# More Strassen pairs in a hybrid encoder block: six further gate and up pairs, an earlier feed of their weight sums, and one gate projection moved to the start

## The chip, the cores and the metric

The kernel runs on one core of a Trainium2 chip, in one launch. The metric is the device time of an execution in microseconds (us). TensorE multiplies matrices, ScalarE (ACT), VectorE (DVE) and GpSimd (POOL) work on elements, SyncE (SP) issues most transfers; ACT and POOL issue some as well. Each of them works through its own instructions in order.

## The reference, cut to what matters

One residual block over 512 frames of 1024 channels, float32:

```python
h = rmsnorm(x, norm1_w)
q, k, v, z, b_raw, a_raw, glu, gates = split(h @ w_in)      # q, k, v, z: 8 heads of 128
q, k, v = silu(causal_conv(concat(q, k, v), dn_conv_w))     # kernel of 4; then q, k l2-normalised
beta, g = sigmoid(b_raw), -exp(A_log) * softplus(a_raw + dt_bias)
o = gated_delta_rule_chunked(q, k, v, g, beta)              # recurrence over time, per head
out_a = (rmsnorm(o) * silu(z)) @ dn_w_o
c = causal_conv(ga * sigmoid(gb), cm_dw_w)                  # kernel of 31
out_b = silu(layernorm(c)) @ cm_w_pw2 + cm_b_pw2
x = x + (sigmoid(gates_a) * out_a + sigmoid(gates_b) * out_b) @ w_out
f_gate, f_up = split(rmsnorm(x, norm2_w) @ w_gate_up)       # 1024 -> 2 x 2816
x = x + (silu(f_gate) * f_up) @ w_down
return rmsnorm(x, norm_f_w)
```

## The kernel before

Activations lie with channels on the 128 partitions and the 512 frames along the free dimension. Every weight is read as float32 and split in two parts, whi and wlo (ScalarE rounds, VectorE takes the rest), and so is every activation (hh and hl). A product of one weight block is three matmuls: high by high, high by low, low by high (`split3`, line 118). `unit` (line 105 loads, 108 and 109 split) prepares 128 x 1024 weight values; its buffers raw, whi and wlo are three deep each.

Stages in order of time:

1. **Start (to 46 us).** x and the first weights come in slices. While the norm's row sums are still unknown, the first GLU products and the 16 columns for beta and decay run on un-normalized inputs uh and ul, and are scaled by the row factor rsb afterwards (`early`, lines 216 to 291). Then xt is scaled by rsb and split into hh and hl (lines 297 to 300), from which all later projections of w_in are made.
2. **Heads and gates (46 to 474 us).** Per head, three projections with a convolution of 4 (`conv4`), one for the gate z, and the preparation of the recurrence (`front`, `front2`, with a substitution `y` on GpSimd, lines 454 and 456). Projections are Python generators that give way after every eighth of a block; `count` counts these steps, eight for a projection. `step` works through a queue: a head, then some steps of `others` (GLU blocks, later the 16 output gates). Beside it run `chains`: `decays` (the cumulated decays and their matrices), and from `START + 32 * nh + ...` on the recurrence of head nh (`chain`).
3. **Output projections, w_out, second norm (474 to 616 us).**
4. **Gate and up projections, 22 pairs of 128 hidden channels.** The first F0 = 10 pairs are plain (48 matmuls of 512 columns each, `col_tile`); the last 12 are Strassen's seven products of half-size blocks (84 matmuls of 256 columns, `pair`, `hprod`). For those the activations are combined beforehand in 11 steps (`todo`), done behind the plain pairs, and the weights' combinations are four sums s1 to s4 per pair, kept in DRAM.
5. **Down projection (848 us to the end)**, also Strassen's products, with sums `wsum` of its weights' blocks.

The sums s1 to s4 are made by transfers alone. `feed` is the list of them in the order of need. `feed_one` issues one copy from SP, behind the last weight load, and, two copies later, an accumulating transfer from POOL. `fill` runs inside `unit` while `start_feed` is true, which is from count 335 on, and with it the loads of half blocks for `wsum` (`half_load`, into the tile "U" that `front` also uses), which POOL adds up:

```python
units[0] += 1
if units[0] % 3 != 2 or not gps_:
    feed_one()
if taken and units[0] % 3 != 2 and not norming[0]:
    dsums_add(*taken.pop(0))
```

`gps_` is empty in stages 4 and 5, so there every unit feeds. What is left of `wsum`'s halves is loaded by POOL in stage 4 (`dsums_to`). The compiler's scheduler orders the instructions of each engine by program order, priorities and its estimate of when operands are ready; `issue_after` and `behind` put an instruction behind a named one of its engine.

Of the kernel before, what the change touches and what calls it, by code (L numbers as in the profile page):

```python
# [6 lines left out]
F32 = mybir.dt.float32  # L7
F32R = mybir.dt.float32r
I32 = mybir.dt.int32
AF = mybir.ActivationFunctionType  # L10
# [13 lines left out]
PAD3 = 368  # L24
START = 84
ROUND = 40
# [5 lines left out]
def block_kernel(ctx, tc, a):  # L32
# [111 lines left out]

    FK, F0 = FF // 2, 10
    sums = {n: dram.tile([FF - F0, P, T], F32, name=n, bufs=1) for n in ("s1", "s2", "s3", "s4")}
# [62 lines left out]
    with tc.tile_pool(name="st", bufs=2) as st:  # L209
# [7 lines left out]
                 for p, kw in ((wp, {}), (wp, {}), (st, {}), (st, {}))]  # L217
        nc.sync.dma_start(vec, a["vec"])
        nc.scalar.dma_start(ident, a["cst"][:, 0:P])
# [5 lines left out]
        for q in range(4):  # L225
            nc.sync.dma_start(xt[:, 2 * q, :], a["xt"][2 * q])
            load(0, q)
            nc.sync.dma_start(xt[:, 2 * q + 1, :], a["xt"][2 * q + 1])
            if q == 0:
                nc.sync.dma_start(wb, a["wba"])  # L230
            for u in (1, 2):
                load(u, q)
        xtok = pa_.tile([P, NT, D], F32, name="A")
# [11 lines left out]
        wbh, wbl = wbhl[:, :, 0, :], wbhl[:, :, 1, :]  # L245
        V.tensor_copy(out=wbh, in_=wb)
        V.tensor_tensor(out=wbl, in0=wb, in1=wbh.bitcast(F32), op=ALU.subtract)

# [3 lines left out]
        for k in range(KD):  # L252
            w = vec[:, k:k + 1]
            S.activation(uh[:, k, :], xt[:, k, :], AF.Copy, scale=w)
            V.scalar_tensor_tensor(out=ul[:, k, :], in0=xt[:, k, :], scalar=w, in1=uh[:, k, :].bitcast(F32),
                                   op0=ALU.mult, op1=ALU.subtract)
            if k % 2 == 0:
                c = slice(k * P, k * P + 256)
                for raw, hi, lo in early[:3]:
                    S.activation(hi[:, c], raw[:, c], AF.Copy)  # L260
                    V.tensor_tensor(out=lo[:, c], in0=raw[:, c], in1=hi[:, c].bitcast(F32), op=ALU.subtract)
            c = slice(k * P, k * P + P)
            for (_, hi, lo), ps in zip(early[:3], eps_):
                split3(ps, (hi[:, c], lo[:, c]), uh[:, k, :], ul[:, k, :], k == 0, k == KD - 1)
            PE.matmul(bps[0:32, :], wbs[:, 32 * k:32 * k + 32], uh[:, k, :], start=k == 0, stop=False)
            PE.matmul(bps[0:16, :], wbs[:, 32 * k:32 * k + 16], ul[:, k, :], start=False, stop=k == KD - 1)
        ss = st.tile([P, 2, NT], F32, name="rms_ss", bufs=1)
# [13 lines left out]
        for k in range(KD):  # L281
            c = slice(k * P, k * P + P)
            split3(eps_[3], (hi[:, c], lo[:, c]), uh[:, k, :], ul[:, k, :], k == 0, k == KD - 1)
        def glu0(i):
            sg = tp.tile([P, T], F32, name="sg")
# [21 lines left out]
        for n in range(NT):  # L307
# [26 lines left out]
        V.scalar_tensor_tensor(out=sp, in0=ax, scalar=0.0, in1=sp, op0=ALU.max, op1=ALU.add)  # L334
        V.tensor_tensor(out=g, in0=sp, in1=nea.rearrange("p (a h) -> p a h", a=1).broadcast_to([P, NT, H]),
                        op=ALU.mult)
        V.tensor_scalar(out=eb, in0=eb, scalar1=1.0, scalar2=None, op0=ALU.add)
        V.reciprocal(out=beta, in_=eb)
        V.tensor_scalar(out=nbeta, in0=beta, scalar1=-1.0, scalar2=None, op0=ALU.mult)


# [36 lines left out]

    zall = pa_.tile([P, H, T], F32, name="A")
    junk = tp.tile([P, T], F32, name="pa", bufs=1)  # L380
# [320 lines left out]
    def decays():  # L701

        yield 2
        gps = psg.tile([P, 4, P], F32, name="g")
# [16 lines left out]
    def head(h, done):  # L721
# [14 lines left out]
        v_ = yield from v  # L736
        pz = yield from proj(24 + h)
        z_ = zall[:, h, :]
        S.activation(z_, pz, AF.Silu)


# [27 lines left out]
    while step() or chains:  # L769
        start_feed[0] = count[0] >= 335  # L770
        if nh < H and count[0] >= START + 32 * nh + sum(OTHERS[:nh]):
            chains.append([0, chain(*done[nh])])
            nh += 1
        for c in list(chains):
            if c[0] <= count[0] or not queue:
                with behind():
                    n = next(c[1], None)
                if n is None:
                    chains.remove(c)
                else:  # L780
                    c[0] = count[0] + n
# [227 lines left out]
    def some_operands(f):  # L1009
        if not ff:  # L1010
            fxs.close()
            ff.append(ctx.enter_context(tc.tile_pool(name="ff", bufs=FK)))
        for _ in range(3 if f < F0 else 2):
            if len(made) <= f:
                operands(len(made))
                made.append(1)

    def next_todo():
        if todo:
            with behind():  # L1020
                todo.pop(0)()

    for f in range(F0):
# [8 lines left out]
        sg = fq.tile([P, T], F32, name="cw", bufs=2)  # L1032
        S.activation(sg, pg, AF.Silu)
        if f:
            next_todo()
            pu = psm.tile([P, T], F32, name="mm")
# [4 lines left out]
        tt(hidden(), pu, sg, ALU.mult)  # L1041
        if f:
            next_todo()
        if f > 6:
            some_operands(f)

# [250 lines left out]
```

## Time and profile before

| | |
|---|---|
| three executions | 960.74, 963.14, 963.42 us; median 963.14 |
| profiled execution | 964.17 us, span 961.9 us, granted TensorE clock 0.998 |
| TensorE matmul busy | 98% of the span |
| VectorE, ScalarE, GpSimd busy | 76%, 55%, 37% |
| moved by transfers | 177.39 MB, mean 184 GB/s |
| stage 4, plain part | about 635 to 727.5 us |
| stage 4, Strassen pairs | 727.5 to 848.4 us |

The span is from the first to the last instruction of the profiled execution; its time is 2.3 us longer. Rows of the trace give start, length, engine, line, operation and the tiles written and read; in brackets the idle time before it and what ended it. "PEld" is TensorE's weight load, "SPq" an issue by SyncE. A DMA share is the mean busy share of the core's 16 DMA engines.

### The profile page before, as it was taken

To read this page: it belongs to the slowest core of one execution; us is meant where nothing else is said; L and a number is where in the kernel's file an instruction comes from. 1 tells how busy PE (TensorE), PEld (TensorE's weight loads), DVE (VectorE), ACT (ScalarE), POOL (GpSimd) and SP (SyncE) were. 2 spreads that over 40 slices of the span, in tenths; PEclk is the share of its full clock that TensorE was granted. 3 is DMA by queue.
4 is the path that set the end of the run, shared out by engine and by line. 5 is a ranking of instruction groups with operands and counts; after the bars stand their busy time and mean duration, and the time that the engine had idled before them with its cause. 6 is when DMAs were issued, how large, how long until landed. Compare 5 with 4: busy or idle time off the path is not lost.

```text
span 961.9 us, 14869 instructions
## 1 busy us (share of the span) xinstructions
PE 941.8 (98%) x5199; PEld 793.8 (83%) x5199; DVE 731.8 (76%) x1118; ACT 529.4 (55%) x1095; POOL 357.4 (37%) x565
## 2 busy tenths in 40 slices
PE   6999999999999999999999999999999999999996
PEld 5687888888887887888887888888889999988885
DVE  4898888988888888888477763676525887889886
ACT  6588865867856775544547232423324545556554
POOL 0323645243463327534345342245451111134034
PEclk9999999999999999999999999999999999999999
DMA  9243423133231426988897985499899556578653
GB/s 310 94 143 101 123 66 92 59 116 102 66 103 55 129 82 176 279 253 248 257 297 221 288 277 175 174 272 281 294 252 224 191 184 193 174 221 268 212 192 134
DMA packets 78298, 177.39 MB, mean 184 GB/s; under 512 B 10208, under 2 KB 19328, under 8 KB 77200
## 3 DMA queue, kind: packets, MB, share of 16 engines
q1 hardware_dynamic: 66816, 144.88, 45.4%
q0 software_dynamic: 10256, 28.89, 13.3%
q10 hardware_dynamic: 1152, 2.69, 0.7%
q8 instruction: 41, 0.67, 0.3%
q14 instruction: 33, 0.27, 0.1%
HBM read 156.22 MB, written 45.37 MB: 210 GB/s over the span
## 4 chain that ended last, share of the span: by engine, by line
PE 90%; DVE 4%; ACT 2%; POOL 2%; issue 1%; DMA 1%; SPq 0%; POOLq 0%; ACTq 0%; DVEq 0%
PE mm L118 59%; PE w L118 20%; PE g L385 1%; PE st L564 1%; PE g L418 1%; PE st L558 1%; DVE wlo L109 1%; PE b L490 1%; PE st L563 1%; PE b L496 1%; DMA gsl<-sgd 1%; POOL ss L879 1%; PE b L514 1%; PE st L552 1%; PE g L467 1%
## 5 line engine op out<-in xcount | busy, mean ns | idle before, releaser
L108 ACT ACTIVATE whi<-raw 128x1024 fp32r<-128x1024 f32 (+1 forms) x191 | 196.4, 1030 | 246.8 <-PE mm L118 151.1
L109 DVE TENSOR_TENSOR wlo<-raw,whi 128x1024 fp32r<-128x1024 f32 (+1 forms) x191 | 242.3, 1270 | 95.9 <-ACT whi L108 95.3
L118 PE MATMUL mm<-hh,whi 128*128 128x512 f32 (+1 forms) x688 | 269.9, 393 | 0.5 <-ACT whi L108 0.3
L118 PE MATMUL mm<-hl,whi 128*128 128x512 f32 (+1 forms) x688 | 264.0, 384 | 2.3 <-POOL hl L300 1.6
L118 PE MATMUL mm<-hh,wlo 128*128 128x512 f32 (+1 forms) x688 | 263.9, 384 | 0.1
L620 DVE SCALAR_TENSOR_TENSOR cps<-c,c31w,cps 128x512 f32<-128x512 f32 x240 | 180.2, 751 | 4.3
L118 PEld LDWEIGHTS mm<-hl,whi 128*128 128x128 f32 x688 | 129.9, 189 | 24.7 <-POOL hl L300 2.9
L118 PEld LDWEIGHTS mm<-hh,wlo 128*128 128x128 f32 x688 | 129.6, 188 | 23.8 <-DVE wlo L109 0.6
L118 PEld LDWEIGHTS mm<-hh,whi 128*128 128x128 f32 x688 | 129.8, 189 | 22.7 <-ACT whi L108 0.8
L949 POOL TENSOR_TENSOR fm<-fm 128x256 f32<-128x256 f32 x33 | 29.8, 904 | 113.3 <-DVE s L949 90.1
L372 DVE SCALAR_TENSOR_TENSOR acc<-mm,c4w,acc 128x511 f32<-128x511 f32 (+2 forms) x72 | 53.0, 738 | 1.9 <-ACT acc L369 1.9
L118 PE MATMUL mm<-yh,whi 128*128 128x512 f32 x128 | 50.7, 396 | 0.0
L118 PE MATMUL mm<-yl,whi 128*128 128x512 f32 x128 | 50.0, 391 | 0.6 <-DVE yl L808 0.6
L454 POOL TENSOR_TENSOR ytm<-U,y 128x60 f32<-128x60 f32 (+14 forms) x120 | 31.8, 265 | 48.6 <-DMA U<-sc 30.9
L118 PE MATMUL mm<-yh,wlo 128*128 128x512 f32 x128 | 49.8, 389 | 0.0
L118 PE MATMUL w<-hh,wlo 128*128 128x256 f32 x168 | 47.7, 284 | 0.3 <-DVE wlo L109 0.3
L118 PE MATMUL w<-hh,whi 128*128 128x256 f32 x168 | 47.6, 284 | 0.0
L118 PE MATMUL w<-hl,whi 128*128 128x256 f32 x168 | 47.5, 283 | 0.0
L118 PE MATMUL w<-wlo,fh 128*128 128x512 f32 (+1 forms) x115 | 44.3, 385 | 0.2 <-DVE wlo L109 0.2
L118 PE MATMUL w<-whi,fl 128*128 128x512 f32 (+1 forms) x115 | 44.2, 384 | 0.0
L118 PE MATMUL w<-whi,fh 128*128 128x512 f32 (+1 forms) x115 | 44.2, 384 | 0.0
L456 POOL TENSOR_TENSOR y<-y,ytm 128x60 f32<-128x60 f32 (+14 forms) x120 | 39.0, 325 | 9.4
(324 smaller groups left out, 1904.0 us busy)
## 6 DMA issues: line engine op xcount, KB each, us to landing
raw<-in_win_dram SPq DMA_DIRECT2D x61, 512.0 KB, 3.5
raw<-in_wgu_dram SPq DMA_DIRECT2D x32, 512.0 KB, 3.5
s<-in_wgu_dram SPq DMA_DIRECT2D x48, 256.0 KB, 6.2
raw<-s SPq DMA_DIRECT2D x48, 256.0 KB, 3.8
raw<-wsum SPq DMA_DIRECT2D x44, 256.0 KB, 4.0
raw<-in_wdn_dram SPq DMA_DIRECT2D x33, 256.0 KB, 3.3
s<-in_wgu_dram POOLq DMA_DIRECT2D x24, 256.0 KB, 6.9
s<-s POOLq DMA_DIRECT2D x24, 256.0 KB, 7.0
```

What stands on the lines that cost most here:

```text
L108: marked(S.activation(hi, raw, AF.Copy), "unit")
L109: marked(V.tensor_tensor(out=lo, in0=raw, in1=hi.bitcast(F32), op=ALU.subtract), "unit")
L118: marked(PE.matmul(ps, l, r, start=first and i == 0, stop=last and i == 2))
L372: marked(V.scalar_tensor_tensor(out=acc[:, s:], in0=ps[:, :T - s], scalar=c4w[:, j, k:k + 1], in1=acc[:, s:], op0=ALU.mult, op1=ALU.add))
L385: PE.transpose(ps[:, n, :], src[:, n, :], ident)
L418: PE.matmul(ps[:, n, :], kT[:, n, :], kT[:, n, :], start=True, stop=True)
L454: G.tensor_tensor(out=tm[:, :, 0:w], in0=U[:, k, :, k + 1:], in1=y[:, :, k:k + 1].broadcast_to([P, NT, w]), op=ALU.mult)
L456: last[0] = G.tensor_tensor(out=y[:, :, k + 1:], in0=y[:, :, k + 1:], in1=tm[:, :, 0:w], op=ALU.add)
L467: PE.matmul(ps[:, n, :], kT[:, n, :], qT[:, n, :], start=True, stop=True)
L490: PE.matmul(ps[:, n, 0:16], Ud[:, n, :], xc[:, n, 0:16], start=True, stop=True)
L620: V.scalar_tensor_tensor(out=acc, in0=c[:, k:k + T], scalar=c31w[:, i, k:k + 1], in1=acc, op0=ALU.mult, op1=ALU.add)
L949: return eng.tensor_tensor(out=out, in0=in0, in1=in1, op=op)
```

## The change

- The last 18 pairs instead of the last 12 are Strassen's (F0 = 4), so four sums each for six more pairs are made: 72 feeds instead of 48. `start_feed` is true from count 112 on instead of 335.
- The 11 combinations of activations go into the four plain pairs: two slots a pair, and as many at the first slot as would not fit otherwise. The hidden blocks' operands for the down projection are made from the first Strassen pair on, up to two a pair.
- Head 0's gate projection (weight block 24) runs at the start on uh and ul; its result is scaled by rsb and goes through silu after the decay inputs. Head 0 is one projection shorter.
- The load of `vec` goes from SP's queue to ACT's; the load of the 16 beta and decay columns goes behind the other first weights, and their products are made two eighths later.
- `decays` waits for 12 counts instead of 2; recurrences start at 80 instead of 84, and four counts sooner again from head 1 on.

```diff
-START = 84
+START = 80
...
-    FK, F0 = FF // 2, 10
+    FK, F0 = FF // 2, 4
...
-        nc.sync.dma_start(vec, a["vec"])
+        nc.scalar.dma_start(vec, a["vec"])
...
             nc.sync.dma_start(xt[:, 2 * q + 1, :], a["xt"][2 * q + 1])
+            for u in (1, 2):
+                load(u, q)
             if q == 0:
                 nc.sync.dma_start(wb, a["wba"])
-            for u in (1, 2):
-                load(u, q)
...
-        V.tensor_copy(out=wbh, in_=wb)
-        V.tensor_tensor(out=wbl, in0=wb, in1=wbh.bitcast(F32), op=ALU.subtract)
...
-            PE.matmul(bps[0:32, :], wbs[:, 32 * k:32 * k + 32], uh[:, k, :], start=k == 0, stop=False)
-            PE.matmul(bps[0:16, :], wbs[:, 32 * k:32 * k + 16], ul[:, k, :], start=False, stop=k == KD - 1)
+            if k == 1:
+                V.tensor_copy(out=wbh, in_=wb)
+                V.tensor_tensor(out=wbl, in0=wb, in1=wbh.bitcast(F32), op=ALU.subtract)
+            for b in [k - 2] if 1 < k < KD - 1 else [k - 2, k - 1, k] if k > 1 else []:
+                PE.matmul(bps[0:32, :], wbs[:, 32 * b:32 * b + 32], uh[:, b, :], start=b == 0, stop=False)
+                PE.matmul(bps[0:16, :], wbs[:, 32 * b:32 * b + 16], ul[:, b, :], start=False, stop=b == KD - 1)
...
+        zps = pst.tile([P, 4, P], F32, name="st").rearrange("p n t -> p (n t)")
+        hi, lo = unit(a["win"][24])
+        for k in range(KD):
+            c = slice(k * P, k * P + P)
+            split3(zps, (hi[:, c], lo[:, c]), uh[:, k, :], ul[:, k, :], k == 0, k == KD - 1)
+        zall = pa_.tile([P, H, T], F32, name="A")
...
+        with tc.issue_after(g_.ins):
+            V.tensor_tensor(out=zall[:, 0, :], in0=zps, in1=rsb, op=ALU.mult)
+        S.activation(zall[:, 0, :], zall[:, 0, :], AF.Silu)
...
-        yield 2
+        yield 12
...
-        pz = yield from proj(24 + h)
         z_ = zall[:, h, :]
-        S.activation(z_, pz, AF.Silu)
+        if h:
+            pz = yield from proj(24 + h)
+            S.activation(z_, pz, AF.Silu)
...
-        start_feed[0] = count[0] >= 335
-        if nh < H and count[0] >= START + 32 * nh + sum(OTHERS[:nh]):
+        start_feed[0] = count[0] >= 112
+        if nh < H and count[0] >= START + (32 * nh - 4 if nh else 0) + sum(OTHERS[:nh]):
...
-        for _ in range(3 if f < F0 else 2):
+        for _ in range(2):
...
     def next_todo():
-        if todo:
+        slots[0] -= 1
+        while len(todo) > slots[0]:
             with behind():
                 todo.pop(0)()
+
+    slots = [2 * F0]
...
+        next_todo()
         if f:
-            next_todo()
             pu = psm.tile([P, T], F32, name="mm")
...
-        if f:
-            next_todo()
-        if f > 6:
-            some_operands(f)
+        next_todo()
```

More of the change, by code (lines that the diff above doesn't have):

```diff
@@ L334, in block_kernel @@
         V.scalar_tensor_tensor(out=sp, in0=ax, scalar=0.0, in1=sp, op0=ALU.max, op1=ALU.add)
-        V.tensor_tensor(out=g, in0=sp, in1=nea.rearrange("p (a h) -> p a h", a=1).broadcast_to([P, NT, H]),
+        g_ = V.tensor_tensor(out=g, in0=sp, in1=nea.rearrange("p (a h) -> p a h", a=1).broadcast_to([P, NT, H]),
                         op=ALU.mult)
@@ L377, in conv4 @@
         return o
-    zall = pa_.tile([P, H, T], F32, name="A")
     junk = tp.tile([P, T], F32, name="pa", bufs=1)
```

## The prediction

> **What bounds the kernel now.** I read the page first: the busy row, then the stretches of the span stage by stage, the chain of waits, and the DMA rows.
>
> ```profile
> span 961.9 us, 14869 instructions
> PE 941.8 (98%) x5199; PEld 793.8 (83%) x5199; DVE 731.8 (76%) x1118; ACT 529.4 (55%) x1095; POOL 357.4 (37%) x565
> ...
> L108 ACT ACTIVATE whi<-raw 128x1024 fp32r<-128x1024 f32 (+1 forms) x191 | 196.4, 1030 | 246.8 <-PE mm L118 151.1
> L109 DVE TENSOR_TENSOR wlo<-raw,whi 128x1024 fp32r<-128x1024 f32 (+1 forms) x191 | 242.3, 1270 | 95.9 <-ACT whi L108 95.3
> ```
>
> TensorE is busy 98% of the span, and what splits each weight block for it, ScalarE's whi and VectorE's wlo, mostly waits for TensorE (151.1 of 246.8 us idle). So two things alone can shorten the run: less matmul time, and work placed into the few gaps. Two things can lengthen it: a raw weight block that lands late, and a small wait on the way that the many buffers no longer cover. The 98% comes from modelled ends, so I take prices from distances between starts, in the chain of waits (start, length, what):
>
> ```profile
> 634.98 92.51 PE mm L118 x408
> ...
> 747.64 11.52 PE w L118 x96
> 759.16 2.88 PE mm L118 x24
> 762.04 1.44 PE w L118 x12
> 763.48 4.32 PE mm L118 x36
> 767.80 11.52 PE w L118 x96
> ```
>
> The first row is the plain gate and up projections: 408 matmuls of 512 columns in 92.51 us, 0.2267 us each, without a break. Then come the Strassen pairs: two last 767.80 - 747.64 = 20.16 us, 10.08 each, 84 matmuls of 256 columns at 0.120 us, again without a break. The gaps lie at the start; TensorE and what released it:
>
> ```profile
> 7.22 0.61 PE L265 MATMUL g<-uh,cv 128*32 128x512 f32 x1 [7.22 <-DVE cv L247]
> ...
> 37.08 0.50 PE L118 MATMUL mm<-hh,whi 128*128 128x512 f32 x1
> ...
> 41.34 0.50 PE L118 MATMUL mm<-hl,whi 128*128 128x512 f32 x1 [1.29 <-POOL hl L300]
> 43.59 0.50 PE L118 MATMUL mm<-hl,whi 128*128 128x512 f32 x1 [0.59 <-DVE hl L300]
> 46.29 0.50 PE L118 MATMUL mm<-hl,whi 128*128 128x512 f32 x1 [0.36 <-POOL hl L300]
> ...
> 46.85 0.40 PE L118 MATMUL mm<-hh,whi 128*128 128x512 f32 x1
> ```
>
> The first projection on normalized inputs, head 0's keys, starts at 37.08 and the next one at 46.85: 9.77 us for 24 matmuls that take 24 x 0.2267 = 5.44. It waits for hl, which VectorE and GpSimd produce until 46.2: 4.3 us lost.
>
> **The first gate on un-normalized inputs.** Head 0's gate projection, 24 matmuls, leaves its place among the heads and goes ahead of the key projection, on uh and ul, which are long there. It needs 5.44 us; the key projection then starts near 42.5 and meets hl nearly without waiting, its last eighth at about 42.5 + 7 x 0.68 = 47.3, behind 46.2. It ends near 47.9 instead of 46.85, and 5.44 us are gone later: 4.4 us gained. Its weight load goes one place ahead of the key's on SP, its split takes the place of the key's, and the key's the next, at 29.50, where VectorE had been idle 2.84 us; the query's, third, now has to be ready when the key projection ends:
>
> ```profile
> 29.50 1.22 DVE L109 TENSOR_TENSOR wlo<-raw,whi 128x1024 fp32r<-128x1024 f32 x1 [2.84 <-ACT whi L108]
> ...
> 46.99 1.22 DVE L109 TENSOR_TENSOR wlo<-raw,whi 128x1024 fp32r<-128x1024 f32 x1
> ```
>
> It was done at 48.2 and is needed at about 48.3: I book 0.2 us. The scaling by rsb that the gate's result now needs is one more VectorE pass of 0.7 us behind the decay inputs; VectorE has background convolution steps to put off there, so nothing.
>
> **The start.** The small vector goes to ACT's queue, so SP issues the first activations 0.45 us sooner (ScalarE computes nothing yet); the beta weights go behind the other weights, their two products are put off to k = 2 and later.
>
> ```profile
> 0.73 0.40 SPq L218 DMA_DIRECT2D vec<-in_vec_dram  x1
> ...
> 1.18 0.42 SPq L226 DMA_DIRECT2D xt<-in_xt_dram  x1
> ...
> 6.07 0.40 ACT L260 ACTIVATE whi<-raw 128x256 fp32r<-128x256 f32 x1
> ```
>
> Before, TensorE's first instruction waited until 7.22 for VectorE's split of the beta weights, although whi was ready at 6.47. Now it waits for whi alone, at about 6.0. The bounds are 0.45 us (SP's issue) and 1.2; VectorE's ul, the second matmul's operand, comes at 6.5, so I take 0.8. TensorE runs unbroken from there to 36.6, so it carries through. The first gains sum to 4.4 + 0.8 - 0.2 = 5.0 us.
>
> **Decays later, recurrences sooner.** The same instructions at other places in the order. In the chain of waits the decay products stood behind this row, without a gap:
>
> ```profile
> 46.29 15.27 PE mm L118 x66
> ```
>
> A later priority moves them little. Recurrences start 4 counts sooner, with 7 counts of work gone ahead of them in head 0: nearly the same place. Nothing, covered by buffers; up to 2 us if not.
>
> **Six more Strassen pairs.** 10.88 - 10.08 = 0.80 us each, 4.8 us in TensorE time. The eleven combinations of activations now have to fit into four plain pairs, four of them at once in the first; VectorE was idle 4.17 us there, and is half idle in that stage (49.39 of 92.5 busy, below). I book 0.2.
>
> ```profile
> 630.28 1.23 DVE L109 TENSOR_TENSOR wlo<-raw,whi 128x1024 fp32r<-128x1024 f32 x1 [4.17 <-ACT whi L108]
> ```
>
> **Their sums.** There are 72 feeds instead of 48, each a DRAM copy of 256 KB from SP and an accumulating transfer of 256 KB from POOL. I count the places: in the heads and gates from count 112 on 45 weight units, two thirds of them feed: 30; in the two output projections and w_out 21 units: 14; in the plain pairs 1 + 2 + 2. That makes 49 before the first Strassen pair, so 23 fall on units of the first six pairs, one per unit, four per pair. Before, only five did. This is the disputed step. What the transfers did: stretches with the busy time of PE, PEld, DVE, ACT and POOL, the clock, the DMA share and GB/s, then the queues of 635 to 727.5 and of 717 to 737.6.
>
> ```profile
> 180.00:230.00 50.00, 50.00 (x287) 41.31 (x286) 45.31 (x87) 38.17 (x104) 19.49 (x43) 1.00 0.28 91
> ...
> 380.00:446.00 66.00, 65.52 (x355) 53.74 (x355) 60.12 (x103) 31.02 (x75) 30.02 (x39) 1.00 0.88 258
> 635.00:727.50 92.50, 92.50 (x410) 76.57 (x410) 49.39 (x44) 29.39 (x40) 44.03 (x38) 1.00 0.91 273
> 717.00:727.50 10.50, 10.50 (x49) 8.71 (x48) 4.42 (x5) 3.62 (x6) 3.30 (x4) 1.00 1.05 253
> 727.50:737.60 10.10, 10.10 (x86) 10.10 (x86) 4.93 (x7) 3.25 (x6) 2.46 (x3) 1.00 1.01 243
> 767.80:808.00 40.20, 40.20 (x337) 40.20 (x337) 32.17 (x49) 19.90 (x28) 6.16 (x8) 1.00 0.58 183
> ```
>
> ```profile
> q0 software_dynamic: 3174, 11.29, 48.1%
> ...
> raw<-in_wgu_dram SPq DMA_DIRECT2D x14, 512.0 KB, 3.6
> ```
>
> ```profile
> q0 software_dynamic: 1039, 1.88, 57.9%
> q1 hardware_dynamic: 1615, 3.21, 45.1%
> ...
> raw<-s SPq DMA_DIRECT2D x5, 256.0 KB, 5.5
> ```
>
> In the last window (20.6 us, full) POOL's queue q0, all accumulations, took 57.9% for 1.88 MB: 1.66 us of all engines for one of 0.262 MB. SP's q1 took 45.1% for 3.21 MB: 0.76 us for a copy, 5.3 us for one pair's 1.835 MB of weights. A pair with four feeds thus asks for 5.3 + 4 x (0.76 + 1.66) = 15.0 us of DMA in 10.08 us; at 1.05, the largest share in a row, 14.3. The first five units and their copies are issued in the plain stage already (as SP did before, up to 724.63), so 18 units, 4.5 pairs, are left: 4.5 x 4.2 = 19 us. A raw block is issued 9 us before its use (758.79 for the pair at 767.80), lands in 3.6 and is split in 1.03 + 1.27, so 3.1 us are slack; two accumulations, 3.3 us, trail behind the last unit. Upper end: about 13 us of stall.
>
> ```profile
> 758.79 3.00 SPq L105 DMA_DIRECT2D raw<-in_wgu_dram  x2
> ...
> 724.63 0.50 SPq L189 DMA_DIRECT2D s<-in_wgu_dram  x1
> ```
>
> Lower end: 0, since a transfer cannot land before it is asked for and no work leaves this stage. For it: accumulations lead their use by eleven pairs and may slip; what must be in time is 5.3 + 3.0 = 8.3 us, below 10.08. With q0 at 48.1% raw blocks landed in 3.6 us, with a full fabric in 5.5, hardly over the slack, and TensorE did not wait in 717 to 737.6. I take 5.5 us, nearer to these landings than to the full sum.
>
> The Trainium skill (DMA: Bandwidth & Descriptors, Queues, rings and completion order) says that each DMA engine takes its queues in turn, packet by packet. By that rule accumulations do not slip behind the weights, and the sum would hold the upper end, 13 us, in place of 5.5. The trace speaks half for it: landings rise from 3.6 to 5.5 us when q0 is busiest.
>
> **The heads under the feed.** From count 112 on (some 125 us) units also load halves of the down weights' sums, 21 instead of 8, into the buffers that the heads' U uses, and POOL adds them (the plain stage is rid of its four in return).
>
> ```profile
> L169 POOL TENSOR_TENSOR U<-U 128x256 f32<-128x256 f32 x32 | 28.8, 901 | 16.4 <-DMA U<-in_wdn_dram 14.7
> ...
> L193 POOL DMA_DIRECT2D s<-in_wgu_dram x8 | 7.6, 988 | 15.7 <-DMA s<-in_wgu_dram 15.7
> ```
>
> 13 more halves at 4 x 0.90 us and 18 more accumulations at 0.99: 65 us more on POOL between 125 and 474. TensorE needs POOL in time once a head: y.
>
> ```profile
> 251.77 0.21 POOL L456 TENSOR_TENSOR y<-y,ytm 128x4 f32<-128x4 f32 x1
> ...
> 266.71 0.40 ACT L481 ACTIVATE yb<-y,cst 128x64 f32<-128x64 f32 x1
> ```
>
> Here it had 15 us in hand. Between 380 and 446 the same halves and feeds ran at a DMA share of 0.88 with 65.52 of 66.00 us busy. SP, in order, will wait longer for a free U, and raw loads stand behind it, several units ahead. I book 0.6 us; 8 if POOL's backlog eats the 15.
>
> **Sum.** -5.0 - 4.8 + 0.2 + 0.6 + 5.5 = -3.5 us on the profiled execution of 964.17 us (span 961.9 and 2.3 around it): 960.7. That execution lies 1.0 us above the median of the three, 963.14, so 959.6 is the forecast. About 0.3%, 2.9 us, is what a measurement here can tell from no change.
>
> **Rivals.** (1) The feed stays hidden altogether: 964.2 - 9.8 + 0.8 - 1.0 = 954. For it: no TensorE wait at shares of 1.05 and 1.01. Against: those 20 us held two copies; the new pairs hold eight in that time. 0.25. (2) The other side: equal turns of the two queues, so that the first six pairs run at the pace of the DMA engines, about 14 us each: 13 us stall, 967; with the saturated durations and no slack, 19 us, 973. It decides from a stall of 9 us on, where all gains are gone. For it: 15.0 us asked for in 10.08. 0.18. By the Trainium skill's rule of turns it is this one. (3) POOL's backlog in the heads: y late by more than the 15 us, some heads stall, 8 us in all, together with 5.5: 967. Against: POOL was busy 19.5 of 50 us there. 0.08. (4) The early gate gains nothing, because its split pushes hl back by as much: 964. Against: VectorE idled 2.84 us in front of 29.50. 0.07. The forecast has 0.42, with a range of its own of 955 to 965.
>
> **Chances and range.** Faster: rival 1 and over half of the forecast's, 0.48. Same: two fifths of the forecast's, rival 4, a little of 2: 0.25. Slower: rivals 2 and 3 and a rest: 0.27. The range reaches from rival 1 to beyond the upper end of the stall, 952.5 to 970.
>
> **What would show it.** A first matmul near 6.4 and no gap of TensorE over 0.5 us between 30 and 47 would bear out the 5.0. Twelve undisturbed pairs of 10.08 us at the end and six before them, whose length is the question: 10.1 is rival 1, 11 the forecast, 13 and more rival 2, with ScalarE's whi waiting for raw transfers and a DMA share at 1.0. In the heads TensorE's share says whether POOL matters: ScalarE's L481 waiting for y L456 would be rival 3. The forecast is wrong if pairs with feeds run at another pace than between 10.5 and 12 us, or if a stage that I left unchanged, the output projections or the down projection, moves by more than 2 us.

## The result, and the profile after

The changed kernel takes 1022.63 us (median of five, 1021.52 to 1024.56) against 963.14 us: 1.062 times the kernel before, 95% interval 1.060 to 1.064. It is 59 us slower; the forecast was 3.5 us faster. Its profiled execution has a span of 1020.9 us.

Where the 59 us lie is read from the chain of waits, at four landmarks that both kernels have: the second-to-last unbroken block of the heads' stage (120 matmuls), the first gate and up block (45), and the down projection (135). First before, then after:

```profile
446.63 27.25 PE mm L118 x120
616.75 5.83 PE w L118 x45
848.44 30.63 PE w L118 x135
```

```profile
501.65 27.24 PE mm L118 x120
670.70 5.82 PE w L118 x45
907.79 30.62 PE w L118 x135
```

Up to the first landmark 55.0 us are lost; from there to the gate and up blocks 1.1 are won (170.12 against 169.05), in the gate and up stage 5.4 lost (231.69 against 237.09), and from the down projection to the end 0.3 won. So nearly all of it is in the heads, where the prediction booked a gain of 4.4. Each landmark comes from one profiled execution, and these lie between 1.5 us below and 3.4 us above the median of their run (before 1.0 above), so single differences of 1 to 3 us should not be read closely. Two stretches of the heads show how the time goes (busy us of PE, PEld, DVE, ACT, POOL, then the granted clock, the DMA share and GB/s). Before:

```profile
130.00:230.00 100.00, 99.81 (x572) 81.66 (x572) 88.81 (x169) 71.46 (x196) 36.24 (x85) 1.00 0.26 82
230.00:380.00 150.00, 149.70 (x896) 121.62 (x894) 127.69 (x251) 101.30 (x296) 71.49 (x170) 1.00 0.33 100
```

After:

```profile
130.00:230.00 100.00, 86.55 (x460) 70.10 (x459) 81.00 (x148) 69.72 (x191) 51.84 (x120) 0.88 0.36 108
230.00:380.00 150.00, 140.90 (x842) 115.79 (x842) 107.21 (x219) 110.06 (x319) 113.30 (x217) 0.97 0.64 176
```

TensorE, which stood still for 0.2 us here, now does so for 13.5 of the first 100 us, and its mean granted clock is 0.88; 460 matmuls are done in place of 572. No other engine is full (GpSimd, the fullest riser, is busy 113.30 of 150 us): the engines wait for one another. GpSimd shows where it begins. The decay matrix of head 0, DT, is made at (before, after):

```profile
69.70 3.79 POOL L393 TENSOR_TENSOR DT<-DT,cst 128x512 f32<-128x512 f32 x3
```

```profile
147.81 2.69 POOL L405 TENSOR_TENSOR DT<-DT,cst 128x512 f32<-128x512 f32 x2 [77.93 <-DMA DT<-mrow]
```

GpSimd waited 77.93 us for the transfer out of mrow, and head 0's recurrence, which needs DT, with it. (The lines of the changed kernel lie 12 further down.) Two steps back in the order, mrow is filled from a small copy by ScalarE, mr = mrt[0:32, 0:P]. Before it stood at 62.74; after it is at 138.29:

```profile
62.74 0.27 ACT L716 ACTIVATE cv<-g 32x128 f32<-32x128 f32 x1
```

```profile
137.79 0.60 ACT L634 ACTIVATE cv<-cps 128x512 f32<-128x512 f32 x1 [6.09 <-DVE cps L632]
138.29 0.25 ACT L728 ACTIVATE cv<-g 32x128 f32<-32x128 f32 x1
```

Its operand was there long before; the product that makes it ran at 57.74:

```profile
57.74 0.41 PE L726 MATMUL g<-cst,cv 128*32 128x128 f32 x2
```

What stands directly in front of the copy is the end of the second background convolution of 31 taps, which writes a tile named cv too. cv is a ring of eight buffers that thirteen tiles share, mrt among them. By the code, "yield 12" has the second background convolution written down in the program ahead of mr; with "yield 2" mr came first.

### The profile page after: what moved, and what is told of

Read it like the earlier page. It is cut to its first block, busy times and chain, and to the rows that moved or that the text cites. A ratio compares the mean times of both kernels' runs of the same rounds, so it can differ in the third digit from the quotient of the medians.

```text
span 1020.9 us, 15556 instructions
## 1 busy us (share of the span) xinstructions
PE 958.0 (94%) x5415; PEld 819.2 (80%) x5415; DVE 752.7 (74%) x1161; ACT 548.9 (54%) x1118; POOL 370.3 (36%) x605
## 4 chain that ended last, share of the span: by engine, by line
PE 64%; POOL 13%; DMA 9%; DVE 4%; ACT 4%; issue 4%; SPq 1%; POOLq 0%; ACTq 0%; DVEq 0%
PE mm L118 39%; PE w L118 20%; POOL U L169 3%; DMA raw<-s 3%; DMA wsum<-U 3%; POOL y L468 2%; POOL ytm L466 2%; DVE wlo L109 2%; DMA U<-sc 1%; SPq L452 1%; ACT whi L108 1%; POOL s L193 1%; POOL Un L434 1%; POOL ss L891 1%; DMA U<-in_wdn_dram 1%
## 5 line engine op out<-in xcount | busy, mean ns | idle before, releaser
L108 ACT ACTIVATE whi<-raw 128x1024 fp32r<-128x1024 f32 x203 | 206.6, 1019 | 256.5 <-PE mm L118 140.5
L109 DVE TENSOR_TENSOR wlo<-raw,whi 128x1024 fp32r<-128x1024 f32 x203 | 247.7, 1221 | 99.8 <-ACT whi L108 98.4
L118 PE MATMUL mm<-hh,whi 128*128 128x512 f32 (+1 forms) x620 | 241.7, 390 | 2.6 <-ACT sg L616 1.5
L118 PE MATMUL mm<-hh,wlo 128*128 128x512 f32 (+1 forms) x620 | 239.1, 386 | 1.5 <-DVE wlo L109 1.5
L118 PE MATMUL mm<-hl,whi 128*128 128x512 f32 (+1 forms) x620 | 236.7, 382 | 0.0
L169 POOL TENSOR_TENSOR U<-U 128x256 f32<-128x256 f32 x84 | 67.5, 804 | 25.8 <-DMA U<-in_wdn_dram 22.1
L193 POOL DMA_DIRECT2D s<-in_wgu_dram x36 | 32.1, 891 | 102.2 <-DMA s<-in_wgu_dram 102.2
L118 PE MATMUL w<-hh,wlo 128*128 128x256 f32 x228 | 65.3, 286 | 3.0 <-DVE wlo L109 2.8
L193 POOL DMA_DIRECT2D s<-s x36 | 30.7, 853 | 88.1 <-DMA s<-in_wgu_dram 60.5
L466 POOL TENSOR_TENSOR ytm<-U,y 128x60 f32<-128x60 f32 (+14 forms) x120 | 36.2, 302 | 44.4 <-DMA U<-sc 35.8
L118 PEld LDWEIGHTS w<-hh,wlo 128*128 128x128 f32 x228 | 43.7, 192 | 4.3 <-DVE wlo L109 4.2
```

The lines of the kernel that those rows point to most:

```text
L108: marked(S.activation(hi, raw, AF.Copy), "unit")
L109: marked(V.tensor_tensor(out=lo, in0=raw, in1=hi.bitcast(F32), op=ALU.subtract), "unit")
L118: marked(PE.matmul(ps, l, r, start=first and i == 0, stop=last and i == 2))
L169: G.tensor_tensor(out=o, in0=x, in1=y, op=ALU.add)
L193: fed.append(nc.gpsimd.dma_start(*begun.pop(0), accum_op=ALU.add, max_dma_last_dim=2048))
L466: G.tensor_tensor(out=tm[:, :, 0:w], in0=U[:, k, :, k + 1:], in1=y[:, :, k:k + 1].broadcast_to([P, NT, w]), op=ALU.mult)
```

## The experiments

Two theories at the start. **A**: the decays' place, "yield 12", delays mr behind the background convolutions, because both take buffers of the one ring and these are given in program order. **B**: the early feed and the early halves load SP and GpSimd, and the decays are late as one consequence of it (rival 3 of the prediction). The landmark "heads" below is the start of the row of 120 matmuls (the output projections, which the expectations name, start some 33 us later):

| run | heads | time, us | ratio to before (95%) |
|---|---|---|---|
| before | 446.63 | 963.14 | |
| after | 501.65 | 1022.63 | 1.062 (1.060 to 1.064) |
| e1, decays at 2 | 459.89 | 981.04 | 1.018 (1.014 to 1.022) |
| e2, mr in its own buffer | 455.38 | 976.57 | 1.015 (1.012 to 1.018) |
| e3, before, decays at 12 | 468.43 | 986.03 | 1.024 (1.022 to 1.026) |
| e11, as e3, mr in its own buffer | 445.18 | 962.25 | 1.000 (0.999 to 1.001) |
| e4, decays at 2, halves and feed from 335 | 443.00 | 999.18 | 1.038 (1.035 to 1.040) |
| e5, decays at 2, halves from 335 | 450.06 | 986.18 | 1.024 (1.020 to 1.028) |
| e6, decays at 2, feed from 335 | 454.08 | 993.98 | 1.032 (1.027 to 1.036) |
| e10, halves from 335, decays late | 473.78 | 1009.17 | 1.049 (1.047 to 1.051) |

**e1: decays at their old place.** Only the number is undone.

```diff
-        yield 12
+        yield 2
```

> The changed kernel with one number put back: `yield 2` instead of `yield 12` in `decays`. Buffer theory: at count 12 the first two background convolutions have been traced already, their results come from the same eight buffers (cv) as the small copy mr, and mr's first writing is put behind theirs on ScalarE (138.3 us instead of 62.7), so the first decay matrix comes 78 us late and all recurrences with it. Then this run loses nearly all of the 55 us that the heads cost: mr near 60 us, DT on POOL near 68, output projections from about 470 to 478 (529 in the changed kernel, 474 before), 10 us of stall in the six pairs with feeds as in the changed kernel, time 963 to 972. POOL theory (rival): the halves' sums and the feed in the heads hold GpSimd up, and the late decays are only a symptom: output projections still from 510 or later, time 1000 or more.

981.04 us: 42 of the 59 us are gone, and DT is made at 67.5 us. Theory B, by which DT would have stayed late, falls as the main cause. The expected 963 to 972 was missed all the same: the output projections start at 492.9 in place of 470 to 478, so the heads lose something else besides.

**e2: the place kept, the buffer changed.** mr goes into a tile of its own (a padding tile that nothing reads or writes).

```diff
-    base.tile([P, PAD3], F32, name="pad")
+    mrp = base.tile([P, PAD3], F32, name="pad")
...
-        mr = mrt[0:32, 0:P]
+        mr = mrp[0:32, 0:P]
```

> The changed kernel, decays still at count 12, but mr lies in the unused pad tile instead of one of the eight cv buffers. Buffer theory: the copy follows its product at once, near 60 us, and the time is that of the kernel with `yield 2`, within 3 us. If the later place of the decays were itself the cause: DT still comes tens of us late, time above 1000. POOL theory: above 1000 as well.

976.57 us, with "yield 12" in place, 4.5 us below e1 where 3 were allowed. ScalarE's copy is early again:

```profile
59.46 0.26 ACT L728 ACTIVATE pad<-g 32x128 f32<-32x128 f32 x1
```

So it is the shared ring, not the later count, that holds the copy back.

**e3 and e11: the same two edits in the kernel before.** e3 has "yield 12" there, e11 the own buffer as well.

> The kernel before with one number changed: `yield 12` in `decays`, nothing else. Buffer theory: mr behind the second background convolution, DT some 60 to 80 us late, heads 35 to 60 us longer, time 1000 to 1020. POOL theory: no halves and no feed in the first heads here, so within 5 us of before.

> The kernel before with its decays at count 12 (986.0 when they lie in the shared buffers), and now the copy of the decay rows, mr, in the tile pad, a buffer of its own. If the shared buffers' order is the whole cause, the copy stands on ScalarE near 63 to 70, DT on GpSimd near 70 to 77, the output projections start at 479 to 481 and the time is 962 to 965: then moving the decays by ten counts costs nothing by itself. If the later place itself costs (work traced behind count 12 is late on its engines), the time stays between 970 and 986 although the copy's buffer is free.

e3 takes 986.03 us, well short of the expected 1000 to 1020; e11 takes 962.25 us, the time of the kernel before. e3's rows have the same neighbour as after's (ScalarE, then GpSimd), and e11's copy is back:

```profile
136.37 0.60 ACT L622 ACTIVATE cv<-cps 128x512 f32<-128x512 f32 x1 [4.78 <-DVE cps L620]
136.86 0.25 ACT L716 ACTIVATE cv<-g 32x128 f32<-32x128 f32 x1
143.61 2.66 POOL L393 TENSOR_TENSOR DT<-DT,cst 128x512 f32<-128x512 f32 x2 [75.23 <-DMA DT<-mrow]
```

```profile
61.19 0.27 ACT L716 ACTIVATE pad<-g 32x128 f32<-32x128 f32 x1
68.15 3.78 POOL L393 TENSOR_TENSOR DT<-DT,cst 128x512 f32<-128x512 f32 x3
```

Theory A holds. It also leaves a question: late decays cost 23 us in the kernel before (468.43 - 445.18) and 42 in the changed one. Something else of the change makes them dearer.

**e4, e5, e6: the early halves and the early feed, one by one**, all with "yield 2".

```diff
# e4: both from 335
-        start_feed[0] = count[0] >= 112
+        start_feed[0] = count[0] >= 335
# e5: the halves alone from 335
-        if halves and gps_ and units[0] > 3 ...
+        if halves and gps_ and count[0] >= 335 and units[0] > 3 ...
# e6: the feed alone from 335
-        if units[0] % 3 != 2 or not gps_:
+        if (units[0] % 3 != 2 or not gps_) and count[0] >= 335:
```

> The changed kernel with `yield 2` and the feed from count 335 on, as before the change. The heads are then free of feed and halves: what they still cost against the kernel with `yield 2` alone is POOL's share. Buffer theory: output projections within 3 us of that kernel's. POOL theory: sooner by 20 us or more. Both: only 31 feeds before the first pair and 41 on pairs, beside four loads of 1 MB for the down weights' sums, so ten pairs or more run at the pace of the DMA engines, 20 to 40 us longer than undisturbed (10 in the changed kernel), DMA share near 1.0 there; time 975 to 995 by the buffer theory.

> The changed kernel with `yield 2`, the feed from count 112 on, but the halves for the down weights' sums from count 335 on, as before the change. Between the kernels with the feed and halves from 112 and from 335 the output projections began at 492.9 and 476.0 us: 16.9 us of the heads. Halves theory (the halves take the heads' U buffers and 13 x 4 additions of POOL, and SP and the recurrences wait for them): output projections at 476 to 479. Feed theory (POOL waits in order for copies to land, and the recurrences' additions stand behind): still 488 or later. The pairs get four loads of 1 MB again beside the feed, so they are longer than 10 us over the undisturbed 181.4: 15 to 25 over; time 970 to 985 by the halves theory.

> The counterpart: `yield 2`, halves from count 112 on, copies and accumulations only from count 335 on. Halves theory: output projections at 488 to 494. Feed theory: at 476 to 479. If each has a share, the two kernels' delays against 476.0 sum to about 17. Pairs: 41 feeds on pairs but no loads of halves, so 17 or 18 us over the undisturbed length (41 - 5 on pairs at 0.5 us, by the 10 us that 18 of the changed kernel's cost).

The landmark is at 443.00 with neither, 450.06 with the feed, 454.08 with the halves, 459.89 with both (e1): the feed costs 6 to 7 us, the halves 10 to 11, and they add. So each has a share, the case that e6's expectation allowed. The times of e4 and e5 came out above the expected ranges, and e6's pairs took 32 us over the undisturbed length where 17 or 18 were expected. The totals are worse than e1's, since what is not done in the heads comes back in stage 4: feeds that fall on the 18 pairs, and, where the halves are late, loads of 1 MB by GpSimd (wst), which makes up for missing halves there. e4's pairs are up to 19 us long. Issues during its pairs, 660 to 790 us (count, KB each, median us to landing):

```profile
s<-in_wgu_dram POOLq DMA_DIRECT2D x14, 256.0 KB, 10.0
wst<-in_wdn_dram POOLq DMA_DIRECT2D x3, 1024.0 KB, 8.3
```

**e10: why late decays are dearer with the halves.** The changed kernel with the halves from 335 only.

> The changed kernel as it is (decays at count 12, in the shared buffers, feed from count 112), but the halves of the down weights' sums are loaded from count 335 on only. With early decays the halves cost the heads 11 us (494.0 with them alone, wo start 487.1 against 476.0). If the losses add, this is 1022.6 - 11 = 1011 to 1012, with the output projections starting near 523 instead of 534.7. If late recurrences and the halves collide in GpSimd's queue and in the tile U (the theory for why late decays cost 22 us alone in the kernel before, but 42 here), it gains 20 us or more: 995 to 1003, start at 505 to 515. If the halves do not matter once the recurrences are late, 1020 to 1023. The decay matrices stay late, near 145, in all three cases.

1009.17 us. Taking the halves away is worth 27.9 us in the heads when the decays are late (501.65 - 473.78) and 9.8 when they are early (459.89 - 450.06). The time moved by 13 us only, as the halves that are missing come back as transfers of 1 MB in the gate and up stage, which takes 251.15 us in place of 237.09. So 1011 came close for the wrong reason; the output projections start at 506.8, within the 505 to 515 of the second theory, collision, whose time (995 to 1003) was missed. The waits of SP's queue between 125 and 476 us show what collides (line and releaser: us, times, longest), after and then e10:

```profile
SPq L163 <- DMA wsum<-U: 63.3, 11, 10.3
SPq L105 <- DVE wlo L109: 60.8, 15, 6.6
...
SPq L163 <- POOL y L468: 32.7, 4, 13.3
...
SPq L163 <- POOL ytm L466: 11.3, 2, 6.4
```

```profile
SPq L105 <- DVE wlo L109: 111.9, 26, 12.0
...
SPq L163 <- DMA wsum<-U: 14.8, 3, 7.5
...
SPq L163 <- POOL ytm L466: 9.7, 1, 9.7
```

L163 is the load of a half into a buffer of U. U has two buffers, which the heads' `front` uses as well, and SP is in order: in after it stood 107 us for a free U (63.3 + 32.7 + 11.3), against 24.5 without early halves. L105, the weight loads, normally waits for VectorE to release a raw buffer, which is harmless; that wait has halved (60.8 against 111.9), as it would if SP comes to it late. SP's order is one way in which the halves can cost time. GpSimd's own order is another, and the rows do not decide between them. The chain that ended last, by engine, before and after:

```profile
PE 90%; DVE 4%; ACT 2%; POOL 2%; issue 1%; DMA 1%; SPq 0%; POOLq 0%; ACTq 0%; DVEq 0%
```

```profile
PE 64%; POOL 13%; DMA 9%; DVE 4%; ACT 4%; issue 4%; SPq 1%; POOLq 0%; ACTq 0%; DVEq 0%
```

Between 125 and 476 us, 10.0% of after's chain is GpSimd's additions of halves (L169), 7.4% the transfers wsum<-U that free U again, and 13.2% the recurrences' substitution (L466, L468), which GpSimd does as well; in e10 the additions are below 1.4%. Giving the halves buffers of their own, or their additions to another engine, was not tried.

With these runs the heads' 55 us are closed in single steps, each the difference of two landmarks and in this order (the steps depend on each other: the halves cost 9.8 with early decays): 443.00 (start part alone, e4), + 7.1 feed (e5), + 23.7 late decays (e10), + 27.9 halves on top of both (after) = 501.65. Against 446.63 the start part brings 3.6.

**e8, e9: start part and Strassen pairs by themselves.** e8 has the decays at 2, F0 = 10 and everything from 335: only the edits of the start are left. e9 has the decays at 2, the halves from 335, F0 = 4, and a feed on every unit from 112, so that all 72 copies are issued before the pairs.

> What is left of the change with `yield 2`, F0 = 10 and feed and halves from 335: the early gate, the start's transfers, the recurrences' places and the slots. Buffer theory and the predicted start part: 3 to 5 us faster than before, 958.5 to 961; the pairs 10.08 us each. If the start part were worth nothing: 963.

> `yield 2`, halves from 335, and every unit feeds from count 112 on (not two in three): 45 + 21 + 5 = 71 of 72 before the first pair. DMA theory of the pairs (the feed's transfers lengthen them): 17 lengths of 10.08 us apart from those beside the four loads of halves, no wait for raw transfers; the 18 pairs within 4 us of 181.4. If the pairs are long for another reason (operands of the down projection two a pair, the combinations squeezed into four plain pairs): again 12.5 us in the first five. By the halves theory the heads stay at 476 to 480, and the time is 956 to 962.

e8: 965.16 us, 1.002 (1.001 to 1.003). The landmark is at 444.11, 2.5 us sooner than before, but the second to fourth pair take 11.2, 13.6 and 11.5 us between the starts of their first matmuls (counted between ScalarE's copies of the pairs' tile w: 14.1, 12.5 and 11.3). That missed the expected 958.5 to 961. e9: 965.82 us, 1.003 (1.002 to 1.004); six pairs of 10.3 us on average and then 10.08, as the first theory had it, at the price of a landmark at 449.65 and output projections from 482.6 in place of 476 to 480, so that the time missed 956 to 962. Feeding ahead moves the cost from the pairs into the heads.

How the pairs stall is read best in the changed kernel, where 18 copies and 19 accumulations fall on the first pairs. A stretch of the chain of waits, one pair long:

```profile
730.08 7.16 DMA raw<-s
...
737.35 1.07 ACT whi L108
...
741.19 1.15 DVE wlo L109
742.35 0.34 SPq L105
...
742.74 7.25 DMA raw<-s
```

TensorE is not in it any more. A raw load lands after 7.16 us, is split, a raw buffer comes free, and only then SP can issue the next load: 12.66 us from load to load. The first six pairs take 10.1, 10.1, 11.8, 12.5, 12.5 and 13.7 us between the starts of their first matmuls, the others 10.1. The median landing in these pairs of the changed kernel, then in the first pairs of e9, with one accumulation left:

```profile
raw<-s SPq DMA_DIRECT2D x23, 256.0 KB, 7.3
```

```profile
raw<-s SPq DMA_DIRECT2D x24, 256.0 KB, 3.7
```

And the changed kernel's pairs with feeds and without, as stretches:

```profile
716.00:786.00 70.00, 63.45 (x500) 60.60 (x499) 41.09 (x60) 28.20 (x40) 15.44 (x19) 1.00 1.00 284
786.00:906.00 120.00, 120.00 (x1002) 120.00 (x1002) 96.00 (x144) 59.90 (x84) 15.34 (x20) 1.00 0.61 189
```

**e12, e13: every unit feeds from 335 on, with 14 and with 12 pairs** (decays at 2).

```diff
-        if units[0] % 3 != 2 or not gps_:
-            feed_one()
+        feed_one()
```

> Decays at 2, feed and halves from count 335 only as in the kernel before, but every unit feeds, and F0 = 8: 14 Strassen pairs, 56 feeds, of which 18 + 21 + 13 = 52 stand ahead of the first pair. If the stall in the pairs is set by feeds left for them (about 0.55 us each, 10 us for 18), this has at most 2 us of it: 963.1 - 2.5 (start, as in the run of the start alone) - 1.6 (two pairs at 0.8) + 0 to 2 = 959 to 961, pairs of 10.1 to 10.5 us. If the denser feed (one per unit instead of two thirds) costs the heads from 335 to 474 as much as the early feed cost them (7 us), 964 to 967, with the output projections starting at 481 or later instead of 477.1.

> The same with F0 = 10: 12 Strassen pairs, 48 feeds, all of them ahead of the first pair. It differs from the run of the start alone (965.2, with 6 us of stall in its first three pairs, 14.14, 12.59 and 11.31 us long) only in that every unit feeds. If those 6 us come from accumulations issued in the pairs' stage, they go: 959 to 960.5, first pairs of 9.3 to 10.5 us. If they come from something else in the start part (the combinations of activations, or the operands of the down projection made from the first pair on), the pairs stay at 14, 12.6 and 11.3 and the time at 964 to 966.

e12 missed: 967.81 us, 1.006 (1.003 to 1.009), with pairs of 10.7, 12.9 and 12.7 us. Six accumulations and one exchange of 1 MB fall on its pairs. e13 was right about the pairs (10.1 us on average, e8's stall is gone) and wrong about the time, 962.49 us, 1.000 (0.999 to 1.001): from the heads' landmark to the gate and up blocks it takes 171.9 us, e8 169.4. The three runs with the dense feed (e9, e12, e13) take 171.3 to 171.9 us there, all others 168.9 to 170.9, so part of the dense feed is paid there. The stall is not proportional to what is left: in the kernel before, four accumulations in the pairs' stage cost nothing (848.44 - 727.49 = 120.95 us for 12 pairs), nine in e8 some 6 us, six in e12 as much. e8 and e12 have 1 MB transfers beside them on their pairs as well, before has none. Such transfers cost little by themselves (e9's pairs, with several of them and one accumulation, lose 1.3 us), but the two were not varied one by one, so what sets the stall off is not shown.

**e14, e15, e16: the old density, begun earlier.** Decays at 2, halves from 335; 12 pairs fed from 280 and from 200, and 14 pairs fed from 112.

> The start part with decays at 2, F0 = 10 (12 pairs, 48 feeds), halves from 335 only, the feed at its old density of two units in three but from count 280 instead of 335: some 5 accumulations go from the pairs' stage into the heads. If stall and accumulations go together, of the 8 accumulations that cost 6 us in the pairs 3 are left, the stall is 1 to 3 us, the output projections start near 478 (477.1 when fed from 335) and stay at 89.5 us until w_out: 960 to 962. If any accumulation in the first pairs costs as much, the first two pairs stay at 12 us and more and it is 963 to 965.

> The same, with the feed from count 200: some 11 accumulations more ahead of the pairs than from 335, so none is left in them, all pairs 10.08 us. If an accumulation moved into the heads costs 0.3 us there (7 us for the 20 that the feed from count 112 put there), the output projections start at 480 and the time is 961 to 963, as before; if the early feed costs only where it lies on the heads before count 200, it starts at 477 to 478 and the time is 959 to 960.5, faster than the kernel before by 0.2 to 0.3%.

> The start part with decays at 2, halves from 335 only, F0 = 8: 14 Strassen pairs, 56 feeds, from count 112 on at the old density (about 59 places ahead of the pairs, so none is left in them). Against the run with 12 pairs fed from 200 (960.1) TensorE has 1.6 us less to do. If the feed costs the heads by the number of accumulations (about 0.3 us each), eight more take 2.4 us: 960.5 to 961.5, output projections at 480 to 481. If it costs by the stretch that it lies on, as the run with 18 pairs fed from 112 suggests (output projections at 483.1), 963 to 965. If it costs nothing there, 958 to 959, output projections at 478.

e14: 961.92 us, 0.999 (0.998 to 1.000). e15: 960.12 us, 0.9965 (0.9953 to 0.9977), the one version here that is clearly faster than the kernel before. e16: 962.65 us, 1.000 (0.999 to 1.001). All pairs of the three last 10.08 us. The times of e14 and e15 came out as expected, though e14 without the stall of 1 to 3 us; e16's lies between two of its three cases. e15 and e16 differ by two Strassen pairs with their eight feeds, and by the count from which the feed runs (200 and 112); first block of gate and up, then down projection, of e15 and of e16:

```profile
614.40 5.82 PE w L118 x45
846.07 30.63 PE w L118 x135
```

```profile
618.85 5.83 PE w L118 x45
848.94 30.63 PE w L118 x135
```

The stage between is 1.58 us shorter in e16 (231.67 against 230.09), 0.79 per pair, as forecast; but it starts 4.45 us later, and the medians differ by 2.5 us to e16's disadvantage. Of the 4.45 us, 2.9 lie ahead of the heads' landmark (447.94 against 445.05), where e16 has issued 29 accumulations and e15 21. The rest lies behind it, where both issue 15 or 16, and is within what the versions of the old density scatter there. A price per feed does not come out of this. The eight would cost 0.36 us each, and e16's output projections start at 480.9, as for 0.3 us each; but from e8 to e15 eleven more accumulations go ahead of the landmark (10, then 21) for 0.9 us, and e9 with 43 stands where e5 does with 29 (449.65 and 450.06). The feeds that e16 adds ahead of the landmark lie on counts 112 to 200, so where a feed lies may matter more than how many there are; a run that tells the two apart is missing. Of all this the prediction booked no more than a part of the 0.6 us for the heads.

## Why the prediction was wrong

**Decays later: the step that failed.** "A later priority moves them little ... Nothing, covered by buffers; up to 2 us if not." The trace of before was asked what stood around the decay products and how long they took, and both answers were right. It was not asked which buffers they write, and whose turn is ahead of theirs in that ring of eight. Measured: 23 us alone (e3 against e11), 42 to 46 us with the rest of the change (after against e1 and e2). "Covered by buffers" had it backwards: a ring of buffers is also an order. No rival held this.

**The heads under the feed: named, and far too small.** Booked 0.6 us, 8 as rival 3. Measured 16.9 us with early decays (443.00 to 459.89), and 27.9 for the halves alone with late ones. The prediction named it ("SP, in order, will wait longer for a free U, and raw loads stand behind it") but took its price from 380 to 446 us in the trace of before. There no head works in U any more; the last substitution step of before, by its rows' first and last start, is at 372.2:

```profile
L456 POOL TENSOR_TENSOR y<-y,ytm x120: 206/253/1383, 92.3 to 372.2; 128x60 f32<-128x60 f32 x8, 128x56 f32<-128x56 f32 x8, 128x52 f32<-128x52 f32 x8, 128x48 f32<-128x48 f32 x8
```

So the stretch that served as the model lacked the very competitor. The sign that the prediction named, ScalarE waiting for y, did not come; but rival 3's engine was not a bad guess, as GpSimd holds 13% of after's chain against 2% before. How much of the price is GpSimd's order and how much SP's stays open. And the feed alone costs 6 to 7 us (e4 against e5, e6 against e1), for which the same 0.6 us had to do.

**The pairs: 5.5 booked, 10.2 measured.** From 716.14, where the pairs' first row stands in the chain, to 907.79 are 191.65 us for 18 pairs, against 18 x 10.08 = 181.4. The first six pairs took 11.8 us on average, the long ones 11.8 to 13.7, between the forecast (11) and rival 2 (13 and more). In stall, the upper bound of 13 us was the better estimate. By the Trainium skill's rule (DMA: Bandwidth & Descriptors, Queues, rings and completion order), each DMA engine takes its queues in turn. Raw landings of 7.3 us at a DMA share of 1.00 agree with it, though they would not tell it from another way of sharing. The wrong choice was to take the landings of a busy stretch, 5.5 us, for the landings of a full one. e12 bears that out: where its TensorE stands still most, the share is above 1 as well.

```profile
728.00:733.00 5.00, 4.01 (x31) 3.60 (x30) 2.14 (x3) 1.58 (x2) 0.00 (x0) 1.00 1.04 257
733.00:738.00 5.00, 3.59 (x27) 3.08 (x25) 2.02 (x3) 2.25 (x4) 0.81 (x1) 1.00 1.09 283
```

**Six more pairs: right, 0.79 us each** (two pairs, e16 against e15), and with all six in place e9's gate and up stage is 3.5 us shorter than e15's (228.18 against 231.67), 1.3 us of stall included. So the combinations in four plain pairs cost nothing to be seen.

**The start: 5.0 booked, 2.5 to 3.6 measured at the heads' landmark** (444.11 in e8 and 443.00 in e4, against 446.63). Against e11, which has the old start and stands at 445.18, it is 1.1 to 2.2. e15, the start part with an earlier feed, is 3.0 us faster in the median. The signs of the start came true: first matmul at 6.11 (e15), and the stretch 30 to 47 us without a gap:

```profile
30.00:47.00 17.00, 17.00 (x78) 13.83 (x77) 16.99 (x22) 11.51 (x15) 7.66 (x4) 1.00 0.06 23
47.00:62.00 15.00, 13.08 (x55) 10.34 (x54) 13.87 (x33) 10.11 (x18) 2.43 (x8) 0.89 0.38 129
```

Before, 14.70 and 15.00 us were busy in these two. What was won in the first is lost in the second: TensorE comes to the decay products at 54.22, 7.2 us sooner than before (61.40). The last of the small VectorE steps that make their operand, before and in e15, has come only 5.0 us sooner, and TensorE waits for it:

```profile
60.82 0.19 DVE L335 TENSOR_TENSOR cv<-cv 128x32 f32<-128x32 f32 x1
```

```profile
55.85 0.18 DVE L345 TENSOR_TENSOR cv<-cv 128x32 f32<-128x32 f32 x1
```

```profile
56.14 1.05 PE L719 MATMUL g<-cv,cst 128*128 128x32 f32 x8 [1.92 <-issue]
```

The scaling of the gate was booked at nothing "behind the decay inputs"; what was not asked is what those inputs would be late for once the gate is gone from between. Nor is the start at 6.11 all gain: with the old start, e11 begins at 6.33 and e3 at 6.86, where the profiled execution of before had 7.22.

## What to carry to other kernels

Before a step is moved in the program, list the buffer rings it writes to and who else takes a turn in them: an instruction with all operands ready waits for the tile that was written down before it, and a tile of its own can cost 512 bytes and save 46 us. A transfer that is "hidden" still has a price in a stage that keeps TensorE nearly full (6 to 7 us for the early feed here), to be set against what it buys (0.79 us for each pair, four feeds). And a queue that works in order is priced by the longest wait of anything put into it, so ask of each added issue what its destination buffer waits for.

## What was not expected of the hardware

A pause of TensorE of 1.92 us at 54 to 56 us was followed by matmuls at half pace: in e15 one of 512 columns starts every 0.43 us instead of 0.23, at a granted clock of 0.50, until 61 us (a stretch of two microseconds, then TensorE's rows).

```profile
58.00:60.00 2.00, 2.00 (x6) 1.52 (x6) 2.00 (x3) 1.99 (x3) 1.26 (x5) 0.50 0.07 16
```

```profile
58.59 0.63 PE L118 MATMUL mm<-hh,wlo 128*128 128x512 f32 x1
59.01 0.63 PE L118 MATMUL mm<-hh,whi 128*128 128x512 f32 x1
```

So the pause cost 1.92 us and the slow stretch behind it another 1.7: nine matmuls start between 57.45 and 61.15, in 3.70 us in place of 9 x 0.2267 = 2.04. The Trainium skill (TensorE: Matmul & The Clock Gate, Part 1) gives an idle window of about 3.4 us as the condition for the lower clock; the slow stretch here follows a shorter pause. TensorE had only ten small products to do between the pause and 57.45, 3.2 us in all from its last large matmul; whether these count as idle is not shown. The changed kernel, too, has a mean clock of 0.88 in its heads from 130 to 230 us, where TensorE waits often: a wait of TensorE can be dearer than its length.
